# A longer lag between the convolution norm's additions on GpSimd and its sums over channels on TensorE

## The chip, the core and the metric

The kernel runs on one core of one Trainium2 chip. The metric is the device time of one execution in microseconds (us); kernels are compared by the median of several executions. One more execution is recorded by the hardware profiler, and the lines shown below are from that one.

## The reference, cut to what matters

One step of a streaming encoder layer, for a prompt of 2048 frames and a sample of 64 frames with cached keys and values, all in float32 (D_MODEL 1024, CONV_DIM 512, 8 heads of 64, FFN 2816):

```
h = rms_norm(x, norm1_g) * (1 + sc1) + sh1
z = h @ w_in                       # GLU pair | q | k | v | conv gate | attention gate
u = glu_a * sigmoid(glu_b)
y = depthwise_conv31(u) + b_dw
y = silu(layer_norm(y, ln_g, ln_b))          # mean and variance over the 512 channels
conv_out = y @ w_conv_out
o = band attention of RMS-normed q, k and of v, with a relative bias
x = x + gt1 * ((sigmoid(g_conv) * conv_out + sigmoid(g_attn) * (o @ w_attn_out)) @ w_o)
x = x + gt2 * SwiGLU(rms_norm(x, norm2_g) * (1 + sc2) + sh2)
```

The change concerns `layer_norm(y)`: the mean over 512 channels of each frame, and the mean of the squares of what remains.

## The kernel before, in words

**Tiling.** The 2112 frames are cut into four blocks of the first phase (576 frames with the sample, then 512 each). For each block the kernel computes the norm of x (`norm_tile`, 128 frames at a time, transposed by TensorE), then the products with w_in: q, k and v, the GLU pair in four pieces of 128 channels (`glu`), and the gates. Meanwhile the block's depthwise convolution (`convolve`, 31 taps on VectorE for each piece of channels), its norm (`conv_norm`) and its attention (`attend`, one head after another) run beside the next products. Weights are split into a high and a low float32r part, and a product is three matmuls. The first phase ends at about 1.2 ms; then come the merge of the two branches and the FFN.

**The norm of the convolution.** y holds four pieces of 128 channels on the partitions, with up to 512 frames on the free axis. `conv_norm` (from L1287) adds the four pieces on GpSimd into `s` (3 additions), then `total()` sums `s` over its 128 partitions: one float32 matmul with the matrix `ones` into a PSUM tile `pm`. VectorE subtracts `pm` from the four pieces. ScalarE squares them, GpSimd adds the squares into `s`, and a second `total()` gives the sum of squares. ScalarE takes the root, VectorE the reciprocal in four pieces of 128 frames, GpSimd multiplies the four pieces of y by it; after that come ScalarE's tanh, VectorE's gain and bias, a split into two parts, and stores to the scratch array `c_d` in HBM. `conv_norm` runs five times (the sample's 64 frames, then 512 frames of each of the four blocks), which makes ten sums. The profile shows a float32 matmul as two records, so twenty of them.

**What sets the order.** Nothing in the program waits by a clock. When the kernel is built, a planner writes out one order of instructions for each engine, and each engine takes them in that order, waiting by semaphores for what it needs. `Stream` keeps a modelled time for TensorE, VectorE, ScalarE and GpSimd (`load`). Side work is written as generators that stand in lanes, pumped in the order norm tiles, work on q and k, attention, tail (which holds `conv_norm`) and convolution, each time TensorE's modelled time has gone on by `STEP_NS` = 500 ns (`tick`). A generator yields the modelled time from which it may go on; `stream.when("pool")` is the modelled end of what GpSimd has been given, less 200 ns (`LAG`). A lane takes the next step of a generator when that time has passed in TensorE's model. So a number added to the yielded time is a lag: the more of it, the more other matmuls are written ahead of the next step. TensorE's own products are written between the steps. `PE_LAG` = 400 ns is the lag for steps that give work to TensorE after another engine; it stands in `norm_tile` (transposes after the scaling), in `attend` (scores, transposes, products) and at the two sums.

The transposes of x's norm (`pt<-ident,x_t`) wait for `x_t`, which VectorE scales by `r`; `r` is a power of 128 numbers on GpSimd (`r<-t,mhalf`) after squares on ScalarE (`junk`). q's and k's norms (`kn`, in `qk_rows`) work the same way. Attention's scores `sc` are turned by VectorE (with the bias and the maximum) into `pr` and `sm`, ScalarE takes the exponentials, and TensorE transposes the result (`ptp`). The next score tile needs the PSUM bank that VectorE has just read.

All instructions go through one helper, so the profile shows one line number for them (L102); groups are told apart by the names of their tiles.

Of the kernel before, what the change touches and what calls it, by code (L numbers as in the profile page):

```python
# [41 lines left out]
PL_LESS = 9e9  # L42
TT_LESS = 9e9
PE_LAG = 400.0
TURN_LAG = 2500.0
KN_LAG = 5000.0
X_LAG = 8000.0
# [570 lines left out]
def streaming_layer(ctx: ExitStack, tc: tile.TileContext, I, O):  # L618
    nc = tc.nc
    stream = Stream()  # L620
# [104 lines left out]
    def split(hi, lo, src):  # L725
        act.activation(hi, src, AF.Copy)
        stream.after("dve", "act")
        dve.tensor_tensor(lo, src, hi.bitcast(F32), ALU.subtract)
# [6 lines left out]
    def low(hi, lo, src, n, less=0.0):  # L735
        e, name = either(n, less)
        stream.after(name, "act")
        e.tensor_tensor(lo, src, hi.bitcast(F32), ALU.subtract)
        return name
# [38 lines left out]
    def temp(name, shape=(P, 512)):  # L778
        return wk.tile(list(shape), F32, tag="t", name=name, bufs=NT)

    def parts(n=None, shape=(P, 512)):
        return (
            wk.tile(list(shape), F32R, tag="sh", name="part_h", bufs=NS),
            wk.tile(list(shape), F32R, tag="sl", name="part_l", bufs=NS),
        )
# [85 lines left out]
    def mod_columns(pc, R, c6, ct, nh):  # L871


        pc = pc.rearrange("p (e n) -> p e n", e=2)
        for e in range(2):
            pe.matmul(pc[:, e], R[:, e * P : e * P + P], sel, start=True, stop=True)
        stream.after("dve", "pe")
        pc = pc[:, :, 2 * (nh - 1) : 2 * (2 * nh - 1)].rearrange("p e (h s) -> p e h s", h=nh)
        cs = slice(ct, ct + 2 * nh)

        def place(a):
            return a[:, cs].rearrange("p (h e) s -> p e h s", e=2)

        def wide(a):
            return a.rearrange("p (h e) -> p e h", e=2).unsqueeze(3).to_broadcast([P, 2, nh, 2])

        bias = wide(b_ada[:, 8 * c6 + ct : 8 * c6 + ct + 2 * nh])
        gates_of = lambda i: gates_c[:, i].rearrange("p s k -> p k s")
        out = place({0: B1, 1: A1, 3: B2, 4: A2}[c6] if c6 not in (2, 5) else gates_of((2, 5).index(c6)))
        dve.tensor_tensor(out, pc, bias, ALU.add)  # L890
        if c6 in (1, 4):
            dve.tensor_tensor(out, out, wide({1: g1, 4: g2}[c6][:, cs]), ALU.mult)
        elif c6 in (2, 5):
            dve.tensor_scalar(out, out, {2: 0.25, 5: 0.5}[c6], None, ALU.mult)

    def mod_steps():
        for c6, half in MOD_HALVES:
# [3 lines left out]
            stream.at(  # L901
                stream.when("dve") + TURN_LAG, lambda pa=pa, R=R, c6=c6, half=half: mod_columns(pa[:, 2 * P :], R, c6, 4 * half, 2)
            )
# [268 lines left out]
    def norm_tile(lo, t, free):  # L1172
# [8 lines left out]
        dve.tensor_scalar(x_t, x_t, r, None, ALU.mult)  # L1181
        yield stream.when("dve") + PE_LAG
        for g in range(2):
# [83 lines left out]
    def convolve(u, y, ct, b):  # L1267
# [3 lines left out]
        if states:  # L1271
            yield stream.when("dve") + TURN_LAG
        for rows_, e in states:
# [15 lines left out]
    def conv_norm(y, c0, n, t0):  # L1289
        yv = y[:, :, c0 : c0 + n]  # L1290
        yield lambda: not conv.gens
        s = wk.tile([P, 512], F32, tag="ln_s", bufs=1)

        def total():
            ps = ps_g.tile([P, 512], F32, tag="gp", name="pm")
            pe.matmul(ps[:, :n], ones, s[:, :n], start=True, stop=True)
            return ps

        gps.tensor_tensor(s[:, :n], yv[:, 0], yv[:, 1], ALU.add)
        for ct in (2, 3):  # L1300
            gps.tensor_tensor(s[:, :n], s[:, :n], yv[:, ct], ALU.add)
        yield stream.when("pool") + PE_LAG
        pm = total()
        yield stream.when("pe")
        for ct in range(4):
            dve.tensor_tensor(yv[:, ct], yv[:, ct], pm[:, :n], ALU.subtract)
        yield stream.when("dve")
        act.activation(s[:, :n], yv[:, 0], AF.Square)
        for ct in range(1, 4):
            tmp = temp("ln")  # L1310
            act.activation(tmp[:, :n], yv[:, ct], AF.Square)
            yield stream.when("act")
            gps.tensor_tensor(s[:, :n], s[:, :n], tmp[:, :n], ALU.add)
        yield stream.when("pool") + PE_LAG
        pm = total()
        yield stream.when("pe")
        act.activation(s[:, :n], pm[:, :n], AF.Sqrt, bias=eps_t)
        yield stream.when("act")
        for c in range(0, n, P):
            e = min(n, c + P)  # L1320
            dve.reciprocal(s[:, c:e], s[:, c:e])
            yield
        yield stream.when("dve")
        done = []
        for ct in range(4):
            gps.tensor_tensor(yv[:, ct], yv[:, ct], s[:, :n], ALU.mult)
            done.append(stream.when("pool"))
        for ct in range(4):
            yield done[ct]
            tmp = temp("ln")  # L1330
            act.activation(tmp[:, :n], yv[:, ct], AF.Tanh, bias=lnh[:, 4 + ct : 5 + ct], scale=lnh[:, ct : ct + 1])
            yield stream.when("act")
            dve.tensor_scalar(yv[:, ct], yv[:, ct], lng[:, ct : ct + 1], lnb[:, ct : ct + 1], ALU.mult, ALU.add)
            dve.scalar_tensor_tensor(tmp[:, :n], tmp[:, :n], 1.0, yv[:, ct], ALU.add, ALU.mult)
            yield stream.when("dve")
            hi, lo = parts()
            act.activation(hi[:, :n], tmp[:, :n], AF.Copy)
            yield stream.when("act")
            name = low(hi[:, :n], lo[:, :n], tmp[:, :n], n, TT_LESS)

            def store(ct=ct, hi=hi, lo=lo):
                for l, a in enumerate((hi, lo)):
                    nc.sync.dma_start(c_d[l, ct, :, t0 : t0 + n], a[:, :n].bitcast(F32))

            stream.at(stream.when(name), store)
# [52 lines left out]
    def softmax_scale(pr, sm, n, w, on_act):  # L1398
        dve.reciprocal(sm[:n, 3:4], sm[:n, 2:3])
        if on_act:  # L1400
            stream.after("act", "dve")
            act.activation(pr[:n, :w], pr[:n, :w], AF.Copy, scale=sm[:n, 3:4])
        else:
            dve.tensor_scalar(pr[:n, :w], pr[:n, :w], sm[:n, 3:4], None, ALU.mult)
# [90 lines left out]
    def attend(i):  # L1495
# [10 lines left out]
        for t in range(0, nq, P):  # L1506
# [20 lines left out]
            if t + P < nq:  # L1527
                yield free + PE_LAG, SCORE_ROOM
            else:
# [7 lines left out]
        softmax_scale(*tiles[-1], x in ON_ACT)  # L1537
        yield stream.when("act" if x in ON_ACT else "dve") + PE_LAG
        while now["finished"] < i - 1:
# [3 lines left out]
        if x == "s":  # L1543
# [9 lines left out]
            split(ph[:SMP, 2 * SMP : 3 * SMP], pl[:SMP, 2 * SMP : 3 * SMP], pt[:SMP, 2 * SMP : 3 * SMP])  # L1553
            yield stream.when("dve") + PE_LAG
            for j, m in js:
# [71 lines left out]
    for b, stage in ORDER:  # L1627
# [39 lines left out]
        else:  # L1667
# [7 lines left out]
            if stage == 3:  # L1675
                if b == 0:
                    tail.add(conv_norm(y, 0, SMP, 0))
                    tail.add(conv_norm(y, SMP + HIST, QB, SMP))
                else:
                    tail.add(conv_norm(y, 0, QB, lo))  # L1680
# [674 lines left out]
```

## Time and profile before

| | us |
|---|---|
| median of three timed runs (2960.33 to 2962.21) | 2961.91 |
| the profiled execution | 2958.2 |
| its span, from the first to the last instruction | 2956.1 |
| TensorE busy in the span | 2895.5 |
| VectorE, ScalarE, GpSimd busy | 2041.9, 1363.3, 1166.4 |

How to read the lines of the profile: times are from the start of the span. PE is TensorE's matmul, PEld its weight loads, DVE is VectorE, ACT ScalarE, POOL GpSimd, SP the engine that issues most transfers. A line of the timeline gives start and duration in us, the engine, the line, the operation, `out<-in`, partitions x elements and how many instructions stand in the line; in brackets is the idle time of the engine before it, and the instruction whose end released it. A line of the waits gives the sum of such idle times, how many there were, and the longest. A line of the windows gives the stretch and its length, the busy time of PE, PEld, DVE, ACT and POOL in it with the number of instructions, the mean granted clock of TensorE (1.00 is full), the busy share of the transfers and their GB/s. In the slices of the page each digit is a 40th of the span, in tenths.

### The profile page before, as it was taken

The numbers are of one execution on the slowest core, as the hardware profiler recorded it, in microseconds if no ns is written. First come the engines' busy times: TensorE is split into PE (matmuls) and PEld (weight loads), VectorE is DVE, ScalarE is ACT, GpSimd is POOL, SyncE is SP. The second block draws the span as 40 slices with busy tenths as digits, with TensorE's granted clock in tenths as the row PEclk, the third lists the DMA queues.
The fourth block names the chain that finished last, engine by engine and source line by source line (L and its number), as shares of the span: only waits on it lengthen the run. The fifth ranks groups of instructions, "written<-read, shape, count | busy, mean of one in ns | idle before, by whom it ended". The sixth has DMA issues, their size and how long they took to land.

```text
span 2956.1 us, 44848 instructions
## 1 busy us (share of the span) xinstructions
PE 2895.5 (98%) x16193; PEld 2587.1 (88%) x16193; DVE 2041.9 (69%) x3648; ACT 1363.3 (46%) x2453; POOL 1166.4 (39%) x753
## 2 busy tenths in 40 slices
PE   8999899999999999999999999999999999999999
PEld 5899777787888788888999998999999999999998
DVE  5897687668857885577777746676666547566666
ACT  3345633661465257464433345444444345444442
POOL 1101310111011103454566452366667742465767
PEclk9999999999999999999999999999999999999999
DMA  9988889988987889985444776332333965333333
GB/s 320 320 291 293 285 277 299 286 260 275 303 277 221 277 248 286 280 293 172 150 152 146 261 256 228 99 118 93 114 122 104 332 223 185 97 96 111 115 107 126
DMA packets 467066, 628.04 MB, mean 212 GB/s; under 512 B 36196, under 2 KB 314584, under 8 KB 466845
## 3 DMA queue, kind: packets, MB, share of 16 engines
q1 hardware_dynamic: 452944, 606.11, 63.1%
q10 hardware_dynamic: 13901, 19.08, 1.8%
q8 instruction: 127, 2.08, 0.3%
q14 instruction: 94, 0.77, 0.1%
HBM read 476.53 MB, written 148.54 MB: 211 GB/s over the span
## 4 chain that ended last, share of the span: by engine, by line
PE 48%; DVE 2%; ACT 1%; issue 1%; DMA 0%; POOL 0%; ACTq 0%; DVEq 0%
PE ps L102 29%; PE pd L102 14%; PE pw L102 5%; DVE wlo L102 1%; DVE pw L102 0%; ACT whi L102 0%; DVE ps L102 0%; DVE t L102 0%; DMA tg<-g_d 0%; DVE sums L102 0%; PE pt L102 0%; DVE acc L102 0%; ACT xn L102 0%; DVE hid L102 0%; ACT hid L102 0%
## 5 line engine op out<-in xcount | busy, mean ns | idle before, releaser
L102 PE MATMUL ps<-t,whi 128*128 128x384 f32 (+1 forms) x2112 | 501.7, 322 | 3.0 <-DVE u L102 0.9
L102 POOL TENSOR_TENSOR wlo<-wst,whi 128x1024 fp32r<-128x1024 f32 (+1 forms) x159 | 363.7, 2298 | 243.3 <-ACT whi L102 231.0
L102 ACT ACTIVATE whi<-wst 128x1024 fp32r<-128x1024 f32 (+1 forms) x265 | 258.3, 979 | 321.8 <-PE ps L102 135.0
L102 PE MATMUL ps<-b,whi 128*128 128x384 f32 (+1 forms) x1584 | 381.6, 326 | 6.4 <-ACT early L102 2.7
L102 PEld LDWEIGHTS ps<-t,whi 128*128 128x128 f32 x2112 | 367.7, 188 | 10.2 <-ACT u L102 3.3
L102 DVE SCALAR_TENSOR_TENSOR y<-u,wd,y 128x512 f32<-128x512 f32 (+1 forms) x480 | 369.3, 773 | 6.3
L102 PE MATMUL ps<-hh,whi 128*128 128x512 f32 (+2 forms) x992 | 361.6, 365 | 0.0
L102 DVE TENSOR_TENSOR acc<-acc,pd 128x512 f32<-128x512 f32 x482 | 322.2, 684 | 48.5 <-PE pd L102 46.0
L102 PE MATMUL ps<-hl,whi 128*128 128x512 f32 (+2 forms) x992 | 345.6, 348 | 0.0
L102 PE MATMUL ps<-hh,wlo 128*128 128x512 f32 (+2 forms) x992 | 345.1, 348 | 0.0
L102 PE MATMUL ps<-t,wlo 128*128 128x384 f32 (+1 forms) x1056 | 338.2, 321 | 0.0
L102 PE MATMUL pd<-whi,hid 128*128 128x512 f32 x912 | 297.2, 391 | 0.3 <-DVE hid L102 0.3
L102 PEld LDWEIGHTS ps<-b,whi 128*128 128x128 f32 x1584 | 278.0, 189 | 14.5 <-ACT early L102 4.1
L102 POOL TENSOR_TENSOR r<-t,mhalf 128x1 f32<-128x1 f32 (+2 forms) x68 | 84.1, 1244 | 444.5 <-DVE t L102 434.2
L102 PE MATMUL ps<-b,wlo 128*128 128x384 f32 (+1 forms) x792 | 256.8, 324 | 0.0
L102 ACT ACTIVATE pr<-pr,sm 128x640 f32<-128x640 f32 (+3 forms) x272 | 200.2, 747 | 111.8 <-DVE sm L102 109.2
L102 PEld LDWEIGHTS ps<-hh,wlo 128*128 128x128 f32 x992 | 186.7, 188 | 21.7
L102 PEld LDWEIGHTS ps<-hh,whi 128*128 128x128 f32 x992 | 187.1, 189 | 18.6 <-issue 1.9
L102 DVE TENSOR_TENSOR wlo<-wst,whi 128x1024 fp32r<-128x1024 f32 (+1 forms) x106 | 135.1, 1277 | 98.7 <-ACT whi L102 97.2
L102 PEld LDWEIGHTS pd<-whi,hid 128*128 128x128 f32 x912 | 171.1, 188 | 36.2 <-ACT hid L102 0.7
L102 PEld LDWEIGHTS ps<-hl,whi 128*128 128x128 f32 x992 | 187.5, 189 | 15.5 <-issue 1.4
L102 PEld LDWEIGHTS ps<-t,wlo 128*128 128x128 f32 x1056 | 198.1, 188 | 0.8
(233 smaller groups left out, 6297.4 us busy)
## 6 DMA issues: line engine op xcount, KB each, us to landing
whi<-w_din_h SPq DMA_DIRECT2D x72, 512.0 KB, 6.7
wlo<-w_din_l SPq DMA_DIRECT2D x72, 512.0 KB, 7.5
wst<-sum_d SPq DMA_DIRECT2D x131, 256.0 KB, 2.9
wfo<-in_w_ffn_out SPq DMA_DIRECT2D x64, 512.0 KB, 4.1
wmod<-in_w_ada SPq DMA_DIRECT2D x46, 512.0 KB, 9.0
sum_d<-ws SPq DMA_DIRECT2D x88, 256.0 KB, 2.0
wst<-in_w_ffn_in SPq DMA_DIRECT2D x85, 256.0 KB, 3.3
wst<-in_w_in SPq DMA_DIRECT2D x40, 512.0 KB, 7.6
```

The source lines that it names most:

```text
L102: self.last = f(*args, **kw)
```

## The change

A new constant, 2800 ns, takes the place of `PE_LAG` at the two sums of `conv_norm`, and nowhere else:

```diff
 PE_LAG = 400.0
+SUM_LAG = 2800.0
...
         gps.tensor_tensor(s[:, :n], yv[:, 0], yv[:, 1], ALU.add)
         for ct in (2, 3):
             gps.tensor_tensor(s[:, :n], s[:, :n], yv[:, ct], ALU.add)
-        yield stream.when("pool") + PE_LAG
+        yield stream.when("pool") + SUM_LAG
         pm = total()
...
             gps.tensor_tensor(s[:, :n], s[:, :n], tmp[:, :n], ALU.add)
-        yield stream.when("pool") + PE_LAG
+        yield stream.when("pool") + SUM_LAG
         pm = total()
```

Each of the ten sums is thus written into TensorE's order only when the model has TensorE 2.4 us further along, and everything after it in `conv_norm` with it. As the lanes share one model, other steps (scores, norm tiles, work on q and k, transfers) can change places too. The number of instructions on each engine stays the same; TensorE's order differs in stretches between 257 and 1221 us of the span, and is the same before and after them. GpSimd's order has one change: at about 324 us an `r<-t,mhalf` of a norm tile comes ahead of the four products `y<-y,s` instead of behind them.

## The prediction

> **What bounds the kernel now.** I read the page's head first, then its busy times and slices, then its chain.
>
> ```profile
> span 2956.1 us, 44848 instructions
> PE 2895.5 (98%) x16193; PEld 2587.1 (88%) x16193; DVE 2041.9 (69%) x3648; ACT 1363.3 (46%) x2453; POOL 1166.4 (39%) x753
> PEclk9999999999999999999999999999999999999999
> PE 48%; DVE 2%; ACT 1%; issue 1%; DMA 0%; POOL 0%; ACTq 0%; DVEq 0%
> ```
>
> TensorE works through 98% of the span, at full clock as far as slices of 74 us show. The change issues as many instructions on every engine as before, only in another order, so it can give or cost only what TensorE waits, or what its clock loses in a wait's wake. The next view is therefore TensorE's waits in the stretch that holds all ten sums (250 to 1200 us), and beside it the group of the sums.
>
> ```profile
> PE pt L102 <- DVE x_t L102: 8.2, 3, 5.6
> PE pm L102 <- POOL s L102: 5.6, 4, 1.9
> PE sc L102 <- DVE sm L102: 4.3, 3, 2.4
> PE ps L102 <- DMA whi<-w_dqkv_h: 2.6, 1, 2.6
> L102 PE MATMUL pm<-s,ones x20: 220/592/697, 257.3 to 1128.3; 128*128 128x512 f32 x16, 128*128 128x64 f32 x4
> ```
>
> The columns are the sum, the count and the longest. The sums are the 20 records of the last row (two records each). They wait for GpSimd four times, 5.6 us together: that is all the change can take away where it says it acts. The same engine waits 8.2 and 4.3 us in neighbouring places, where the order moves too, so those must be worked out.
>
> **The change part by part. The sums themselves.** The timeline gives each of the four waits in brackets, and the spacing of what can be put ahead.
>
> ```profile
> 254.93 0.30 PE L102 MATMUL ps<-hl,whi 128*128 128x288 f32 x1
> 255.06 0.29 PE L102 MATMUL ps<-hh,wlo 128*128 128x288 f32 x1
> 257.26 0.43 PE L102 MATMUL pm<-s,ones 128*128 128x64 f32 x2 [1.91 <-POOL s L102]
> 532.80 0.60 PE L102 MATMUL ptp<-ident,pr 128*128 128x128 f32 x4
> 533.15 0.48 PE L102 MATMUL ps<-hh,whi 128*128 128x512 f32 x1
> 533.93 0.39 PE L102 MATMUL ps<-hh,whi 128*128 128x512 f32 x1
> 534.16 0.40 PE L102 MATMUL ps<-hl,whi 128*128 128x512 f32 x1
> 540.39 1.13 PE L102 MATMUL pm<-s,ones 128*128 128x512 f32 x2 [1.27 <-POOL s L102]
> 548.78 0.70 PE L102 MATMUL pm<-s,ones 128*128 128x512 f32 x1 [0.75 <-POOL s L102]
> 813.48 0.70 PE L102 MATMUL pm<-s,ones 128*128 128x512 f32 x1 [1.64 <-POOL s L102]
> ```
>
> Built, the changed kernel gives TensorE the first of these sums 12 matmuls of 128x288 later. Two such starts lie 0.13 apart (254.93, 255.06), so 12 x 0.13 = 1.6 of the 1.91 us goes. The second comes only one group of four transposes later, 0.35 (532.80 to 533.15) of 1.27. The third comes later by more than 20 matmuls of 128x512 (0.23 apart, 533.93 to 534.16), which covers its 0.75 wholly. The fourth comes two groups of transposes and six such matmuls later, 0.7 + 1.4 = 2.1, more than its 1.64. Gain: 1.6 + 0.35 + 0.75 + 1.64 = **4.3 us**. The other six sums wait for nothing now, and are moved behind 3 to 6 us of further matmuls: no gain. What follows a sum (the subtraction, the squares, the second addition, the root, the reciprocals) starts as much later. None of it feeds TensorE before the convolution's result goes to HBM, and in the last block that end has room:
>
> ```profile
> 1168.98 0.63 ACT L102 ACTIVATE part_h<-ln 128x512 fp32r<-128x512 f32 x1 [3.51 <-DMA c_d<-part_h]
> 1186.19 0.63 ACT L102 ACTIVATE part_h<-o_p 128x512 fp32r<-128x512 f32 x1 [0.76 <-DVE o_p L102]
> ```
>
> The norm's last piece leaves ScalarE at 1168.98, attention's last at 1186.19: 17 us of cover, of which a lag longer by 2 x 2.4 us (twice 2800 less 400 ns) takes 5. I put it at nothing; without cover it would be those 5.
>
> **A clock rule.** In the windows round the sums the granted clock is the third column from the right (1.00 is full; behind it stand the DMA share and GB/s).
>
> ```profile
> 250.00:257.00 7.00, 5.35 (x39) 4.98 (x38) 6.96 (x12) 2.26 (x5) 0.09 (x1) 1.00 0.79 236
> 812.00:819.00 7.00, 5.52 (x29) 4.28 (x29) 4.64 (x8) 3.72 (x8) 3.08 (x4) 1.00 0.91 279
> 337.00:346.00 9.00, 4.05 (x12) 3.01 (x13) 6.21 (x19) 6.64 (x16) 3.03 (x2) 0.62 0.99 284
> 409.00:416.00 7.00, 6.64 (x28) 5.53 (x28) 5.97 (x18) 3.66 (x10) 0.00 (x0) 0.76 1.03 345
> ```
>
> The sums' waits of up to 1.9 us leave it at 1.00, so removing them gives their own length only. At 409 us a wait of 2.37 (row below) is followed by 0.76 over 7 us: 7 x 0.24 = 1.7 us lost besides. [...]
>
> **What the moved work meets, block 0 (300 to 415 us).** Here the later reciprocals and products change the order on VectorE and GpSimd.
>
> ```profile
> 318.83 3.39 DVE L102 RECIPROCAL s<-s 128x128 f32<-128x128 f32 x4 [1.32 <-ACT s L102]
> 323.89 4.62 POOL L102 TENSOR_TENSOR y<-y,s 128x512 f32<-128x512 f32 x4
> 328.48 0.54 POOL L102 TENSOR_TENSOR r<-t,mhalf 128x1 f32<-128x1 f32 x1
> 329.05 0.75 DVE L102 TENSOR_SCALAR x_t<-x_t,r 128x1024 f32<-128x1024 f32 x1 [4.91 <-POOL r L102]
> 329.86 0.33 PE L102 MATMUL pt<-ident,x_t 128*128 128x128 f32 x1 [1.28 <-DVE x_t L102]
> 341.83 1.09 PE L102 MATMUL pt<-ident,x_t 128*128 128x128 f32 x4 [5.65 <-DVE x_t L102]
> 408.28 0.69 DVE L102 TENSOR_TENSOR kn<-kn,r 128x512 f32<-128x512 f32 x1 [1.81 <-POOL r L102]
> 409.02 0.28 DVE L102 CUSTOM_DVE_ANT_0 pr<-sc,bias 128x128 f32<-128x128 f32 x1
> 409.36 0.50 PE L102 MATMUL sc<-kk,q 128*128 128x256 f32 x2 [2.37 <-DVE sm L102]
> ```
>
> - At 329.86 TensorE waits 1.28 for x_t, scaled late because r stood behind GpSimd's four products (4.62 us). In GpSimd's new order, its only change, r is ahead of them: the 1.28 goes.
> - At 341.83 the wait of 5.65 stays. The serial chain behind it (score, softmax piece, squares, r, scaled x_t) is the same, but three weight matmuls that lay between two of its score tiles now stand ahead of it. I cost that at +1.0; from 0 to +1.5, about the length of a group as that of the 408.28 wait, is open.
> - At 409.36 the 2.37 us arises because VectorE stands still 1.81 us for r ahead of a kn product, and the 128x128 softmax piece that feeds the next score queues behind it. In the new order that piece stands ahead of the kn product: the 2.37 and the clock's 1.7 go. The product's own transposes come close behind, so I put a new wait of 1.0 (half of 1.81) in: net -3.1, bounds -4.1 and 0.
> - Two lesser places, an x_t at 294.80 that now has an ACT copy ahead of it (+0.3) and a wait at 323.99 that goes (-0.5), nearly cancel:
>
> ```profile
> 294.80 0.66 PE L102 MATMUL pt<-ident,x_t 128*128 128x128 f32 x4 [1.24 <-DVE x_t L102]
> 323.99 0.50 PE L102 MATMUL ps<-wlo,hh 128*128 128x512 f32 x1 [0.52 <-DVE ssq L102]
> ```
>
> Block 0 together: -1.3 + 1.0 - 3.1 - 0.2 = -3.6.
>
> **Blocks 1 to 3.** The order differs in the built kernels at 534 to 679, 813 to 955 and 985 to 1221 us: norm pieces and softmax pieces change places on VectorE, loads of x_t move ahead of a head's q and k on SP's queue, and c_d's stores go later. Beside the sums, nearly nothing is waited for there today, so there is little to win and something to lose. The waits near by that have the same neighbours before and after remain:
>
> ```profile
> 470.33 0.86 PE L102 MATMUL sc<-kk,q 128*128 128x320 f32 x4 [0.93 <-DVE sm L102]
> 472.21 1.17 PE L102 MATMUL sc<-kk,q 128*128 128x320 f32 x3 [1.03 <-DVE sm L102]
> ```
>
> These two show what a softmax piece out of step costs: about 1 us. The trace can't show a wait that doesn't exist yet; one in each of blocks 1 to 3 at that price makes +3, the bounds are 0 and 3 x 2.4 = 7. I take +3, by the nearest rows.
>
> **The sum.** -4.3 - 3.6 + 3 = **-4.9**, say 5 us. The profiled execution took 2958.2 (2956.1 span, 2.1 around it) and would become 2953.3; the median of the three timed runs, 2961.9, stands 3.7 higher, and the same 5 us off it gives **2957**. About 0.2%, 5.9 us, is what a measurement of this kernel can tell from no change, so faster means below 2956.0 and slower above 2967.8.
>
> **The rivals.**
> - **No new waits.** Blocks 1 to 3 take the new order without a gap, and the kn transposes at 409 don't wait. Then -4.3 - 4.6 = -9, and 3 more if the x_t waits that I kept shrink by a third: 2950. It goes from 2955 to 2944, where all of the first three rows of waits (18.1 us) would be gone. For it: GpSimd is busy 39% and VectorE 69%, so later pieces find room. Against it: the 341.83 chain, which is serial and gets no cover.
> - **The sums wait as before.** The second sum moves only 0.35 us although 2.4 us of lag was added, since the lag counts in the planner's modelled time. If the additions themselves come later too, because other moved pieces now stand ahead of them on GpSimd, two thirds of the sums' waits come back: -1.4 stays of the -4.3, and with -3.6 + 3 it makes -2, so 2960. Against it: nine of the ten sums do move by 1.6 us or more, and GpSimd's order has one change only.
> - **Slower: reciprocals in the score chain.** The four reciprocals of a prompt block are 3.39 us of VectorE (row at 318.83). A sum that comes later drops them between softmax pieces of a head, whose next score tile waits for VectorE. A hold of VectorE by 1.81 us made the wait at 409.36: 2.37 and 1.7 of clock, 4.1 us. Once more in each of the four blocks is 16.3; without the gain at 409, and with the -4.3 of the sums and block 0's small terms (-0.5) it is +11.5, so 2973, 2965 to 2978. It decides from two such waits on (8.2 against 4.8 won); one is paid by what is won. For it: in block 0 the new order on VectorE does put pieces of s between softmax pieces. Against it: the planner's reciprocals come one at a time (0.85 us each), and attention runs a head ahead in most places.
>
> **How the numbers follow.** Forecast 2957, own range 2953 to 2961: chance 0.40, of which 3/8 (0.15) lies below 2956.0. No new waits: 0.28, all faster. Sums wait as before: 0.14, same. Reciprocals: 0.18, of which 0.14 above 2967.8. Faster 0.15 + 0.28 = 0.43; same 0.25 + 0.14 + 0.04 = 0.43; slower 0.14. The range 2946 to 2966 leaves out the lower 2 of the second case's 11 us (0.05) and nearly all of the last case (0.15): 2 in 10.
>
> **What would show it.** Right: the group of the sums waiting for GpSimd falls from 5.6 to about 1.2 us, with 0.9 of it left at 540 us; no wait and full clock at 409; an x_t wait of 6 to 7 us at about 340 with the clock dip still behind it; a few waits of about 1 us for VectorE in blocks 1 to 3. Wrong: new waits for softmax sums or ScalarE's exponentials of 2 us or more with a clock below 0.9 (as in the windows 337 and 409) round them (the slower rival); or the 8.2 us of x_t waits grown by more than 2; or the DMA waits for w_dqkv, 2.6 us now, grown because SP's queue holds c_d's later stores ahead of them.

## The result, and the profile after

The changed kernel takes 2964.17 us (median of 20 runs, 2957.58 to 2970.35), the kernel before 2959.59 us in the 20 runs beside them (2955.8 to 2964.55). The ratio is 1.0015, 95% interval 1.0009 to 1.0022: **slower by 0.15%, about 4.5 us** (2.7 to 6.5). That is within the 0.2% called "no change" ahead of the result, but its sign is clear, and it is the wrong one: 5 us less was forecast. That the time lies inside the stated range of 2946 to 2966 is no merit of the forecast. Single runs of one kernel spread over 9 to 13 us here, so one profile against another proves little; what follows rests on medians and on waits that come back in several profiles.

The page's head and busy times of the changed kernel's profiled execution (2966.55 us):

```profile
span 2964.7 us, 44824 instructions
PE 2900.8 (98%) x16193; PEld 2588.6 (87%) x16193; DVE 2045.1 (69%) x3648; ACT 1364.6 (46%) x2453; POOL 1166.4 (39%) x753
```

The counts of instructions with a duration are the same. TensorE is 5.3 us longer busy (2900.8 against 2895.5) with the same matmuls: those ran slower. TensorE's waits between 250 and 1200 us (sum, count, longest):

```profile
PE pt L103 <- DVE x_t L103: 8.6, 2, 5.6
PE sc L103 <- DVE sm L103: 6.2, 7, 1.3
PE ptp L103 <- ACT pr L103: 2.6, 2, 1.8
...
PE pm L103 <- POOL s L103: 1.6, 2, 1.3
```

The sums did what was forecast: their wait for GpSimd fell from 5.6 to 1.6 us. The 4.0 us came back as waits for `sm` (4.3 to 6.2) and for `pr` (0.6 to 2.6). The timeline shows where each stands:

```profile
259.55 0.43 PE L103 MATMUL pm<-s,ones 128*128 128x64 f32 x2 [0.32 <-POOL s L103]
298.35 0.44 PE L103 MATMUL pt<-ident,x_t 128*128 128x128 f32 x2 [2.94 <-DVE x_t L103]
344.99 0.45 PE L103 MATMUL pt<-ident,x_t 128*128 128x128 f32 x1 [5.64 <-DVE x_t L103]
414.66 0.39 PE L103 MATMUL ptp<-ident,pr 64*128 64x64 f32 x3 [1.76 <-ACT pr L103]
548.95 0.70 PE L103 MATMUL pm<-s,ones 128*128 128x512 f32 x1 [1.28 <-POOL s L103]
586.43 0.42 PE L103 MATMUL sc<-kk,q 128*128 128x320 f32 x1 [1.16 <-DVE sm L103]
917.23 0.56 PE L103 MATMUL sc<-kk,q 128*128 128x320 f32 x2 [0.66 <-DVE sm L103]
930.97 0.53 PE L103 MATMUL sc<-kk,q 128*128 128x320 f32 x2 [1.28 <-DVE sm L103]
```

All TensorE gaps over 0.15 us between 240 and 1320 us, added up, make 29.7 us before and 29.0 after. So the waits are even, and the loss is elsewhere: in the clock. (TensorE's order is that of before up to 257 us, yet the two profiles stand 2.3 us apart at 250 us; times of one are set against the other with that taken off.) The windows (third column from the right) round three of these waits:

```profile
296.00:303.00 7.00, 4.65 (x24) 4.65 (x25) 3.98 (x14) 3.74 (x12) 1.65 (x3) 0.76 0.70 175
340.00:350.00 10.00, 5.01 (x14) 4.17 (x15) 7.56 (x22) 7.32 (x16) 2.20 (x2) 0.51 1.03 327
417.00:424.00 7.00, 6.91 (x27) 5.64 (x26) 3.72 (x13) 3.89 (x11) 0.91 (x2) 0.63 1.05 390
```

By the trace's record of the clock, the half-clock stretches of this profile between 200 and 1320 us last 3.4 + 10.2 + 6.8 + 3.4 + 6.8 = 30.6 us, those of the kernel before 6.8 + 4 x 3.4 = 20.4. The granted clock in each of them is 0.50. Ten more microseconds at half clock are 5 us less work. That is no accident of one pair: each run lists its mean granted clock, and it is 0.9945 over 20 runs of the changed kernel against 0.9963 over 119 runs of the kernel before, which is (0.0055 - 0.0037) x 2960 = 5.3 us. The control below, with the order of before, has 0.9960 over 11 runs against 0.9965 beside it, so such a mean over 11 runs can be off by some 1.5 us.

### The profile page after: what moved, and what is told of

Read it like the earlier page. It is cut to its first block, busy times and chain, and to the rows that moved or that the text cites. A ratio compares the mean times of both kernels' runs of the same rounds, so it can differ in the third digit from the quotient of the medians.

```text
span 2964.7 us, 44824 instructions
## 1 busy us (share of the span) xinstructions
PE 2900.8 (98%) x16193; PEld 2588.6 (87%) x16193; DVE 2045.1 (69%) x3648; ACT 1364.6 (46%) x2453; POOL 1166.4 (39%) x753
## 4 chain that ended last, share of the span: by engine, by line
PE 47%; DVE 2%; ACT 1%; issue 1%; DMA 0%; POOL 0%; ACTq 0%; DVEq 0%; POOLq 0%
PE ps L103 29%; PE pd L103 14%; PE pw L103 5%; DVE wlo L103 1%; ACT whi L103 0%; DVE pw L103 0%; DVE ps L103 0%; DMA cin<-o_d 0%; DVE t L103 0%; DVE acc L103 0%; DVE sums L103 0%; PE pt L103 0%; POOL wlo L103 0%; ACT xn L103 0%; DVE hid L103 0%
## 5 line engine op out<-in xcount | busy, mean ns | idle before, releaser
L103 PEld LDWEIGHTS ps<-t,whi 128*128 128x128 f32 x2112 | 367.7, 188 | 10.2 <-ACT u L103 3.3
```

The lines of the kernel that those rows point to most:

```text
L103: self.last = f(*args, **kw)
```

## The experiments

Times are ratios to the kernel before, run beside each kernel, with 95% intervals; 0.001 is 3 us. The lag is chosen by norm (n and t0 are arguments of `conv_norm`) or by sum.

**Control: the changed file with the old lag.**

```diff
-SUM_LAG = 2800.0
+SUM_LAG = 400.0
```

> The changed file with the new constant set back to 400 ns: every engine's order is that of the kernel before, only the line numbers differ. It measures what the comparison itself does. All theories: the same time, -0.7 to +0.7 us in the median, and the same mean granted clock (0.9965, which leaves 10 us of the span's full clock ungranted). If it stands +1 to +3 us, the +2 to +2.6 of the parts run so far are no effect of their orders.

Measured: 1.0001 (0.9992 to 1.0010). The comparison itself adds nothing, and a difference of 0.0009 (2.7 us) is about the least that it can tell.

**The sample's two sums only.** `yield stream.when("pool") + (SUM_LAG if n == SMP else PE_LAG)` at both.

> The longer lag at the sample's two sums only (64 frames in block 0), PE_LAG at the other eight. Its orders are those of the changed kernel up to about 292 us and those of the kernel before behind it. Theory A (the later c_d stores of the sample hold up the x_t loads behind them on SP's queue): the sum at 257 us wins 1.6 us, but the x_t transposes at about 297 us wait near 2.9 us instead of 1.24, with a half-clock stretch of 3.4 us behind, so the profile stands about +2.7 us against the kernel before at 300 us of the span, and the time is +2 to +3.5 us. Rival R (the waits and clock dips differ from run to run and the lag as such costs nothing here): x_t waits about 1.2 to 1.5, no half-clock stretch at 300, time -1 to +1 us.

Measured: 1.0015 (1.0007 to 1.0024), and a mean clock of 0.9951 against 0.9965 beside it: 4.1 us, nearly the whole. The sum won its 1.6 us, and x_t lost more. TensorE's row, and ScalarE's square ahead of it, in this kernel:

```profile
299.86 0.44 PE L103 MATMUL pt<-ident,x_t 128*128 128x128 f32 x2 [4.41 <-DVE x_t L103]
296.37 0.63 ACT L103 ACTIVATE junk<-x_t 128x512 f32<-128x512 f32 x1 [3.19 <-DMA x_t<-in_x_prompt]
```

The square waits for the load of x_t. Why the load is late is seen in the issue times on SP's queue, of the kernel before and of the changed kernel:

```profile
283.22 0.89 SPq L1343 DMA_DIRECT2D c_d<-part_h  x1
284.52 0.86 SPq L1343 DMA_DIRECT2D c_d<-part_l  x1
285.43 3.41 SPq L1150 DMA_DIRECT2D x_t<-in_x_prompt  x3
```

```profile
289.05 0.33 SPq L1344 DMA_DIRECT2D c_d<-part_h  x1
289.81 0.32 SPq L1344 DMA_DIRECT2D c_d<-part_l  x1
290.17 2.67 SPq L1151 DMA_DIRECT2D x_t<-in_x_prompt  x3
```

Right behind the store of the norm's result stand the three loads, in the same order in both kernels. 290.17 against 285.43 is 4.7 us later, and 2.4 with the 2.3 between the profiles taken off. The store holds the loads, but the norm does not hold the store. In the changed kernel the norm's part was ready 8 us ahead of it, and what SP stood for at the store's line (L1344) was a transfer of ScalarE's queue, `g_d<-gate`, issued at 285.02 and landed at 288.98:

```profile
280.80 0.26 ACT L103 ACTIVATE part_h<-ln 128x64 fp32r<-128x64 f32 x1 [0.24 <-DVE ln L103]
SPq L1344 <- DMA g_d<-gate: 2.0, 1, 2.0
```

The semaphore waited for there is the one that tells of that landing and then of the store's own. So the lag did not delay the store by a late result; it gave the store another place among the transfers, and in all six profiles that have the lag at this sum and the stores in this place, the store stood for that landing. In these six the x_t wait was 1.6 to 4.4 us (median 2.8); in the ten without it 1.2 to 2.0 (median 1.24). Theory A holds in that the later stores hold up the loads.

**The same, with the x_t loads ahead of the stores.**

```diff
-            stream.at(stream.when(name), store)
+            stream.at(stream.when(name) + (2500.0 if n == SMP else 0.0), store)
```

> The same, and the sample's stores to c_d are written out 2500 ns later, which puts the three x_t loads ahead of all of them on SP's queue. TensorE's order is that of the sample-only kernel but for 14 records at about 313 us. Theory A: the x_t wait at about 297 us falls to under 0.5 us and no half-clock stretch follows; the 1.6 of the sum and the 1.24 of x_t are both won, so -2 to -3 us against the kernel before. Rival R or any cause other than the queue: x_t still waits over 1.2 us, and the time is like the sample-only kernel's.

Measured: 1.0007 (0.9998 to 1.0016). The wait fell from 4.41 to 1.39, with a second of 0.94 behind it, and the clock there stayed whole:

```profile
297.36 0.66 PE L103 MATMUL pt<-ident,x_t 128*128 128x128 f32 x4 [1.39 <-DVE x_t L103]
302.17 0.33 PE L103 MATMUL pt<-ident,x_t 128*128 128x128 f32 x1 [0.94 <-DVE x_t L103]
297.00:304.00 7.00, 5.69 (x39) 5.23 (x40) 4.53 (x16) 4.00 (x11) 3.14 (x2) 1.00 0.48 120
```

The first load went out at 290.37, against 291.73 in the kernel above: 1.1 us earlier, with 0.3 between these two profiles at 250 us taken off. It did not go out earlier still because SP now stood at this load (L1151) for the same kind of landing:

```profile
SPq L1151 <- DMA g_d<-gate: 3.3, 1, 3.3
```

So the place behind the stores is a cause of the excess, but 1.1 us is less than the 3.0 by which the wait fell. The load also took less time, 3.5 us from its issue to the square that waits for it against 4.6 above, and why is not shown. The landing of `g_d` holds both kernels, and no run moves it. I had the remedy's size wrong: it brings x_t back to what it was, not under 0.5, and two waits for `pr` at about 277 us (1.1 together) eat most of the sum's 1.6. There is no gain in this place, and the intervals of the two kernels overlap.

**Block 0's prompt part only** (`t0 == SMP`).

> The longer lag at the two sums of block 0's prompt part only. Theory A2 (later norm pieces move VectorE's and GpSimd's order, and the softmax pieces wait behind a kn product that stands for r, with longer half-clock stretches): between 300 and 530 us the x_t waits at 324 and 330 go (-1.8), the wait at 409 goes, but one of about 1.8 us for ScalarE's pr ahead of ptp comes in its place, and the half-clock stretches grow from 13.7 to about 20 us: +2 to +4 us. Rival B (what I forecast): -3 to -4 us. Rival R: -1 to +1.

Measured: 1.0014 (1.0005 to 1.0023). My forecast for this part (rival B, -3 to -4 us) fell. TensorE's wait and the VectorE rows that explain it:

```profile
412.83 0.36 PE L103 MATMUL ptp<-ident,pr 64*128 64x64 f32 x2 [1.90 <-ACT pr L103]
409.44 0.69 DVE L103 TENSOR_TENSOR kn<-kn,r 128x512 f32<-128x512 f32 x1 [1.53 <-POOL r L103]
...
412.03 0.15 DVE L103 RECIPROCAL sm<-sm 64x1 f32<-64x1 f32 x1
```

The rows of the kernel before:

```profile
397.76 0.15 DVE L102 RECIPROCAL sm<-sm 64x1 f32<-64x1 f32 x1
404.44 0.69 DVE L102 TENSOR_TENSOR kn<-kn,r 128x512 f32<-128x512 f32 x1 [1.53 <-POOL r L102]
```

The stall of 1.81 us that made the wait at 409 is gone, and the softmax piece stands ahead of its kn product, as forecast. But VectorE also stands for r ahead of the kn product before that one, 1.53 us in both kernels. In the kernel before nothing waited behind that stall, since the reciprocal of another head's `sm` came ahead of it; now it comes behind, and ScalarE's scaling of `pr` and TensorE's transposes follow it. The profile of this kernel has no more half clock here than before, and its profiled execution took 2959.3, so where its 4 us lie is not shown by that one profile. The mean clock of its 11 runs shows what they are: 0.9952 against 0.9965 beside them, (0.9965 - 0.9952) x 2960 = 3.8 us.

**Blocks 1 to 3 only** (`t0 > SMP`).

> The longer lag at the six sums of blocks 1 to 3 only. By the two profiles at hand: block 1 wins about 1 us (sum at 549 and kn at 708), block 2 wins 1.6 at 813 and 1 at 896 and loses 2 to 3 at 917 to 931 (scores behind a kn product that stands for r), block 3 loses about 1.5: together 0 to +2 us. Rival B (what I forecast): 0 to +1 with no score wait over 1.1 us at 917 to 931. Rival C (slower by reciprocals between softmax pieces): +4 us or more, with VectorE's reciprocal ahead of the waiting scores.

Measured: 1.0012 (1.0003 to 1.0021), with score waits of 0.67 and 1.28 at 910 and 924 us as in the changed kernel. The largest wait is in block 1, and VectorE's rows show what holds it:

```profile
577.44 0.85 PE L103 MATMUL sc<-kk,q 128*128 128x320 f32 x4 [2.29 <-DVE sm L103]
575.89 0.69 DVE L103 TENSOR_TENSOR part_l<-ln,part_h 128x512 fp32r<-128x512 f32 x1 [3.80 <-DMA c_d<-part_l]
576.50 0.16 DVE L103 RECIPROCAL sm<-sm 128x1 f32<-128x1 f32 x1
576.58 0.80 DVE L103 CUSTOM_DVE_ANT_0 pr<-sc,bias 128x640 f32<-128x640 f32 x1
```

The norm's low part waits 3.8 us for a buffer, which an earlier store has not left yet; softmax pieces stand behind. It is no reciprocal of the norm: rival C, which I had priced in the prediction, has its collision here but not its cause. The norm's parts and attention's share two buffers, and the lag brought `part_l<-o_p` right ahead of this one.

**All prompt parts, not the sample** (`n != SMP`).

> The longer lag at the eight sums of the four prompt parts, not at the sample's two. Its order is the changed kernel's but for 257 to 292 us. Theory A (each part adds what its own waits and clock dips cost): the full change's +4.6 less the +2 to +3 of the sample, so +2 to +3 us, with the x_t wait at 297 back at 1.2 to 1.5 and no half-clock stretch there. Rival (the parts do not add; the clock's dips come by chance in each run, the more of them the more waits of 1 us or longer there are): +4 to +5.

Measured: 1.0009 (1.0000 to 1.0018), as additive parts would have it. But sample, block 0 and blocks 1 to 3 alone add up to 1.0041, against 1.0015 for the whole. So the parts do not add in the times, though TensorE's order of the whole is in each stretch that of the part. The misfit is in the clock: by the mean clocks the sample loses 4.1 us, block 0 3.8, blocks 1 to 3 2.4 (0.9957 against 0.9965), and the whole only 5.3. Why they do not add stays open.

**Without the wait for r, in both kernels.**

```diff
-    e.tensor_tensor(kn[:n], kn[:n], r.unsqueeze(2).to_broadcast([n, NH, HD]), ALU.mult)
+    e.tensor_tensor(kn[:n], kn[:n], ssq[:n].unsqueeze(2).to_broadcast([n, NH, HD]), ALU.mult)
```

> The kernel before, with the q and k rows multiplied by VectorE's own mean-square tile (ssq) in place of GpSimd's power of it (r): the power is still computed, but the product does not wait for it, so the RMS norm of q and k is not the reference's. Orders are the same but for two TensorE records. Theory K (VectorE standing for r holds the softmax pieces queued behind it): the 2.37 us wait at 409 and the clock dip behind it go, the 1.27 us at 708 shrinks, -4 to -6 us. Rival (r is not what holds them): under -1.5 us and the wait at 409 stays.

> The same edit on the changed kernel (the power of q's and k's mean square is left out of their product). Theory K: the waits at 414 (1.76 us, for ScalarE's pr), 917 (0.66) and 931 (1.28, for VectorE's sm) go with the dip at 415, so it stands 6 to 9 us under the changed kernel, and at 0 to -3 against the kernel before with the same edit. Rival (the loss is only at the sample's x_t at 298 and in block 0's x_t chain): it stands -2 to -4 under the changed kernel, and +3 to +5 over the kernel before with the same edit.

Both kernels leave r out of the norm of q and k, so they do not compute the reference; only their times are of use. Measured: 0.9967 (0.9954 to 0.9979) on the kernel before, 0.9973 (0.9963 to 0.9982) on the changed one. VectorE's standing for r costs the kernel before about 10 us (6 to 14), twice what theory K expected. Its wait at 409 went, that at 708 went, and so did one I had put down to transfers: TensorE waits 3.5 us at 989 to 994 us for w_dqkv loads that stand on SP's queue behind k's stores, which wait for the kn products. The changed kernel gains about 12 us by the same edit; its score waits at 917 and 931 and the `pr` wait at 414 are gone. TensorE's waits in the two (before, then changed):

```profile
PE pm L103 <- POOL s L103: 5.6, 4, 1.9
PE sc L103 <- DVE sm L103: 2.4, 3, 1.0
```

```profile
PE sc L103 <- DVE sm L103: 4.2, 5, 1.1
PE pm L103 <- POOL s L103: 1.6, 2, 1.3
```

Between the two there is +0.0006 left of +0.0015; the intervals do not tell that from nothing, nor from the whole.

**First sums only, second sums only.** `SUM_LAG` at one of the two yields, `PE_LAG` at the other.

> The longer lag at the first sum of each norm only (the mean), 400 ns at the second. Three of the four waits for GpSimd (257, 540, 813 us) are at first sums. Theory L (what costs is that everything behind the second sum comes 4.8 us later and meets x_t loads, the two part buffers and softmax pieces; half the shift costs about half): the sums' waits fall by about 3 us as in the full change, and the losses are half of it: 0 to +2.5 us. Rival M (no relation to the size of the shift: each new order has its own collisions, at other places): the waits named for the full change (414, 586, 917, 931) are gone and others of 0.7 to 2.5 us stand elsewhere; the time anywhere from -3 to +6.

> The longer lag at the second sum of each norm only (the squares). Of the sums' waits only the 0.75 at 549 can go, the 1.9, 1.3 and 1.6 at first sums stay. Theory L: little won, half the losses: +1.5 to +4 us. Rival M: other collisions than in the full change, -2 to +6.

Measured: 1.0023 (1.0014 to 1.0032) and 1.0007 (0.9997 to 1.0016). Half the shift costs as much as the whole or more when it is put at the first sum: theory L (the size of the shift, 0 to +2.5 us there) falls. Rival M stands in the main, though one of the waits that it named as gone stays: `pr` near 414 is 1.56 at 418 in the run of the first sums. The pair of score waits of block 2 is back in block 1, in both kernels (the rows of the first sums; with the second sums 0.67 and 1.28 stand at 632 and 646):

```profile
640.06 0.70 PE L103 MATMUL sc<-kk,q 128*128 128x320 f32 x3 [0.66 <-DVE sm L103]
653.88 0.82 PE L103 MATMUL sc<-kk,q 128*128 128x320 f32 x4 [1.27 <-DVE sm L103]
```

0.66 and 1.28, as at 917 and 931 in the changed kernel: the same alignment of two kn products with two score tiles, in another block.

**Three buffers for the low parts, in both kernels.**

```diff
-    NT, NS = 7, 2
+    NT, NS = 6, 2
...
-            wk.tile(list(shape), F32R, tag="sl", name="part_l", bufs=NS),
+            wk.tile(list(shape), F32R, tag="sl", name="part_l", bufs=NS + 1),
```

> The changed kernel with three buffers instead of two for the low parts (part_l), paid for by six instead of seven scratch tiles of 512 numbers; TensorE's order differs in 40 records only. In the changed kernel VectorE waits 2.7 us (3.8 and 3.5 in two of its parts) at about 582 us for a store of part_l to c_d to land, with two reciprocals and a softmax piece behind it, and TensorE's scores at 586 wait 1.16 (2.29, 1.95). Theory P (the shared ring of two holds VectorE): that VectorE wait goes and the score wait at 586 falls under 0.5, -1 to -2.5 us against the changed kernel, so +2 to +3.5 over the kernel before. Rival (the ring is not what holds, or six scratch tiles cost as much): the wait stays, or +4 to +6 over the kernel before.

> The kernel before (400 ns lag) with three buffers for the low parts and six scratch tiles; TensorE's order is that of the kernel before. If the ring of two is hit only by the longer lag (theory P): -0.7 to +0.7 us, so that of the changed kernel's +4.6 some 3.5 are the ring. If it helps in both alike (rival): -2.5 to -4 us, and the lag costs as much with it as without.

Measured: 1.0003 (0.9993 to 1.0012) on the changed kernel, 0.9997 (0.9988 to 1.0006) on the kernel before. VectorE's wait is gone, and with it that of the scores at 586:

```profile
575.13 0.69 DVE L103 TENSOR_TENSOR part_l<-o_p,part_h 128x512 fp32r<-128x512 f32 x1
575.74 0.68 DVE L103 TENSOR_TENSOR part_l<-ln,part_h 128x512 fp32r<-128x512 f32 x1
```

The ring of two costs the kernel before nothing that can be told and the changed one 0.0012 (3.5 us, from just above 0 to 7). Theory P's mechanism holds: the hold of VectorE and the score wait behind it are the ring's. Its size is less sure, for that score wait is 1.2 of the 3.5 us, and the profiles do not place the rest.

**The lag where it pays.** The ring of three, `SUM_LAG` at both sums of block 1 (`t0 == 576`) and at the second of block 2 (`t0 == 1088`), `PE_LAG` elsewhere.

> The ring of three, the longer lag at both sums of block 1 and at the second sum of block 2, 400 ns elsewhere: the places where the stretches of the profiles so far were shorter than those of the kernel before (block 1 with the ring 2 to 2.5 us, block 2 with the second sum about 2.5 us). Theory (each stretch keeps its price, since TensorE's order differs only there): -3 to -5.5 us against the kernel before. Rival (the prices are chance of single profiles): -1.5 to +2.

Measured: **0.9986 (0.9976 to 0.9996), 2956.94 us, faster than both kernels.** Its stretch from 520 to 720 us is 1.6 us shorter than before, with the second sum of block 1 free of its wait:

```profile
542.89 1.13 PE L103 MATMUL pm<-s,ones 128*128 128x512 f32 x2 [1.27 <-POOL s L103]
555.69 1.02 PE L103 MATMUL pm<-s,ones 128*128 128x512 f32 x2
```

The gain in block 2 (waits for w_dqkv, near 990 us) also varies among profiles of the kernel before's order, so only the total is shown. The places were chosen after the runs above, and the ring is part of the kernel: against the kernel before with the ring alone (0.9997) the lag's own gain is 0.0011, which the intervals do not tell from nothing.

**The kn product later in the order, in both kernels.**

```diff
-        yield stream.when("pool")
+        yield stream.when("pool") + 1500.0
         e, name = either(512, TT_LESS)
         e.tensor_tensor(kn[:n], kn[:n], r.unsqueeze(2).to_broadcast([n, NH, HD]), ALU.mult)
```

> The kernel before, with the product of kn by r written out 1500 ns later than the model's end of GpSimd's power, arithmetic unchanged. Theory K2 (with r there when VectorE comes to it, softmax pieces are no more held): the 2.4 us wait at 409 and the 1.3 at 708 shrink or go, -3 to -8 us. Rival (other steps move with it and collide elsewhere, the transposes of kn among them): -1.5 to +4.

> The same on the changed kernel. Theory K2: waits at 414, 917 and 931 gone, -5 to -10 us against the changed kernel and within 2 us of k0_r1500. Rival: other collisions take their place, +2 to +6 over k0_r1500.

Measured: 1.0025 (1.0016 to 1.0035) on the kernel before, 1.0000 (0.9991 to 1.0008) on the changed one. On the kernel before theory K2 falls, and the loss (+7.4 us) is even above the rival's +4: the wait at 409 shrinks to 1.65 and that at 708 goes, but a row of three new score waits stands in block 2:

```profile
1030.37 0.85 PE L103 MATMUL sc<-kk,q 128*128 128x320 f32 x4 [0.93 <-DVE sm L103]
1032.15 1.33 PE L103 MATMUL sc<-kk,q 128*128 128x320 f32 x4 [0.93 <-DVE sm L103]
1034.40 0.90 PE L103 MATMUL sc<-kk,q 128*128 128x320 f32 x2 [0.93 <-DVE sm L103]
```

These three are 2.8 us, with 6.8 us of half clock from 1032 on in this profile; the stretch from 960 to 1250 us is 5.0 longer than in the profile before. The rest of the 7.4 is not placed. With this edit the longer sum lag makes the kernel *faster*, by 0.0025, where alone it makes it slower by 0.0015. The same lag has either sign, by what it happens to fall beside.

## Why the prediction was wrong, point by point

- **The sums' own gain (-4.3): right.** 1.91 became 0.32 at 257 (1.6 of it, as counted), 0.75 and 1.64 went. Only the 0.35 at 540 did not come: 1.27 stayed 1.28.
- **The waits at 324 and 330 (-1.8): right.** In the changed kernel TensorE waits for nothing between 303 and 338 us.
- **The x_t wait at 341.83 (+1.0): right in size.** It stayed at 5.64, and 0.8 more stands ahead of it at 339, where the three matmuls were.
- **The x_t wait at 294.80 (+0.3): wrong.** It became 2.94, and a half-clock stretch of 3.4 us that was not there follows. The step looked at ScalarE's order alone. On SP's queue the x_t loads stand right behind the moved stores, which stand for a landing of `g_d`; the prediction thought of these stores only for the loads of w_dqkv. The run with the loads put ahead showed the stores' part.
- **The wait at 409.36 (net -3.1): the step that failed.** It said that the wait goes because the softmax piece now stands ahead of the kn product, and that its own transposes wait 1.0 at most. The first half came, and those transposes wait for nothing. But another head's reciprocal fell behind the stall of the kn product before (1.53 us), and TensorE waited for its `pr`: 1.76 in the changed kernel, 1.56 to 2.21 in four others with the lag here. Half clock behind it was 6.8 us where 3.4 had been: -0.6 of wait and +1.7 of clock make about +1 in this profile, where -3.1 was forecast. In the four others half clock behind it was 3.4 us each time, so nothing of the clock's 1.7 came back. With the sample's, this step makes most of the miss: from 250 to 520 us the changed kernel's profile loses 5.8 us on that of before, where -5.2 was forecast.
- **Blocks 1 to 3 (+3): right in the sum of the new waits, by luck.** 1.16, 0.66 and 1.28 came, 3.1 together; the first by the two shared buffers, which I had not named, the others by kn products. Less the sums' gain there (2.7), about +0.3 was forecast for these blocks; the run of them alone measured +3.5 us (0.9 to 6.2), of which 2.4 are clock.
- **The clock.** I counted its loss at one place and as certain. The waits came out even, and the 5 us are what the clock lost. The sum had no term for it elsewhere: in these runs a wait moved to another place cost its length and, where it fell as the last section shows, half clock in pieces of 3.4 us, each 1.7 us of work. That the sums' waits of up to 1.9 us cost no clock was read from one profile (and the window 250 to 257 ends before that wait does): in three of ten profiles with the wait at 257 half clock followed it.
- **The rival "slower"** had the right kind of place (VectorE held ahead of a softmax piece) and the wrong holder, so its price (2973) was far off. The trace agrees with none of the rivals as they were written.

## What to carry to other kernels

In an order written out ahead for several engines, the later step here moved what shares a queue or a buffer with it: the x_t loads went out 2.4 us later behind the norm's stores (the 2.3 between the profiles taken off), and VectorE stood 2.7 us for a buffer of `part_l` in the changed kernel, 3.8 with the lag in blocks 1 to 3 alone. List what stands behind such a step's stores on the transfer queue and who else uses its buffers, before counting the wait that it removes. Look, too, at what a store itself stands for. The stall of VectorE for r took a new victim when the order changed. Leaving r out gained about 10 us on the kernel before and 12 on the changed one; moving the product that waits for r cost 7.4 on the one and gained about 4.5 on the other. Try a lag separately in each place: the whole cost 4.5 us; the picked places, with a third buffer, gained 3 to 4.

## What the runs showed of the hardware

In these profiles half clock came in pieces of 3.41 us at a granted clock of 0.50 (stretches of 3.41, 6.83 and 10.24 us). Their starts in one run lie whole multiples of 3.41 us apart (in the changed kernel 12, 34, 53 and 205 of them behind the first, at 299.33 us), and differently in each run. So one and the same wait was followed by it in some runs only. The score wait of 2.3 to 2.4 us near 410 has the same order ahead of it in seven kernels; three of their profiles show half clock behind it, four do not. One of each, wait and window (the control, then the lag in blocks 1 to 3 alone):

```profile
414.55 0.50 PE L103 MATMUL sc<-kk,q 128*128 128x256 f32 x2 [2.39 <-DVE sm L103]
414.00:421.00 7.00, 6.45 (x25) 5.41 (x26) 5.97 (x19) 3.49 (x10) 0.00 (x0) 0.76 1.04 359
```

```profile
410.15 0.50 PE L103 MATMUL sc<-kk,q 128*128 128x256 f32 x2 [2.37 <-DVE sm L103]
410.00:417.00 7.00, 6.84 (x36) 5.77 (x37) 6.90 (x21) 5.37 (x14) 0.00 (x0) 1.00 1.02 366
```

The sum's wait of 1.9 us at 257 was followed by 3.4 us of half clock in three of ten profiles.

The traces show where half clock followed. Divide each of the 17 profiles between 200 and 1320 us by its own grid of 3.41 us, on which its half-clock stretches start, and add up the time without a matmul in each piece at full clock. Of the 35 pieces with 1.95 us or more, all were followed by half clock; of the 60 with 1.4 to 1.95, 21; of the 5365 with less, one. So in these profiles it was not the single wait that counted but the idle time that fell into one piece, and a wait that the grid parted in two could pass. Near 410 the fullest piece of the three profiles with half clock holds 2.28, 2.38 and 2.39 us, of the four without it 1.18 to 1.83; at 257 it is 1.88 to 1.91 in the three and at most 1.69 in the seven. In the seven profiles the wait near 410 cost its 2.3 to 2.4 us and, in three of them, a half-clock stretch of 3.4 us, 1.7 us of work, more.
